# Seven half-width block products in place of eight for the gate and up projections of a decoder layer

## The chip, the cores and the metric

The kernel runs on one core of one Trainium2 chip. The metric is the device time of one execution in microseconds (us). The engines are TensorE (PE, with its weight loads PEld), VectorE (DVE), ScalarE (ACT), GpSimd (POOL) and SyncE (SP, which here issues DMAs).

## The reference, cut to what matters

One decoder layer on 512 tokens of 1024 features, in float32. Two of its stages are SwiGLU feed-forward blocks with 2816 hidden features; between them lie a projection, two mixers and an output projection, which the change does not touch.

```python
def swiglu_ffn(x, w13, w2):
    gate, up = jnp.split(x @ w13, 2, axis=-1)
    return (jax.nn.silu(gate) * up) @ w2

x = layer_norm(alpha * x + 0.5 * swiglu_ffn(x, ffn1_w13[i], ffn1_w2[i]), ln1_g[i], ln1_b[i])
h = x @ w_in[i]
...
x = layer_norm(alpha * x + mix @ w_out[i], ln2_g[i], ln2_b[i])
ple = jax.nn.sigmoid(x @ ple_gate_w[i]) * (p[i] @ ple_proj_w[i])
x = layer_norm(alpha * x + 0.5 * swiglu_ffn(x, ffn2_w13[i], ffn2_w2[i]) + ple, ln3_g[i], ln3_b[i])
```

## The kernel before, in words

Every float32 operand is split into a high part (a copy rounded to the matmul's input format, on ACT) and a low part (the difference, on DVE); `split` (lines 152 to 154) does this. A product is then three matmuls into one PSUM bank: high x high, high x low, low x high (`mm3`, lines 188 to 192). The input x stands transposed in XH and XL, eight k-tiles of 128 features by 512 tokens.

`ffn` (line 243) runs over 22 hidden tiles of 128 features in groups of 4, 6, 6 and 6. For each tile it makes a gate product and an up product, each 8 k-tiles x 3 matmuls with 512 tokens moving, into PSUM tags a and c (three banks each); `glu` applies silu on ACT, multiplies on DVE and splits the hidden tile. In the first stage's first group the k loop is outside (`k_outer`), so that work starts with the first weights. After a group the second product runs over four token blocks and two halves of 512 output columns: one unit is n x 3 matmuls (n tiles in the group) into PSUM tag b (two banks), and DVE adds it to the residual RES (line 304). After the last group each token block is normalised (`norm_natural`), and in the first stage turned back into XH and XL (`norm_turn`).

Weights come as units of 512 KB through `load` (line 156): SP issues the DMA into one of three raw buffers, ACT copies the high part, DVE subtracts the low part. `ahead` loads the next unit of the list wa (and the four wide ones, wd) whenever one has been used, four units deep; `side` loads one row block of the second product's weights into one of six buffers. Each engine has its own queue and takes its instructions in the order that is fixed when the kernel is built; that order follows the code but is not the code's own, as instructions that would wait are passed by others. In the second stage the gate products of the per-layer embedding (`gate`, `project`) come first.

Of the kernel before, what the change touches and what calls it, by code (L numbers as in the profile page):

```python
# [8 lines left out]
F32 = mybir.dt.float32  # L9
# [7 lines left out]
P = 128  # L17
# [6 lines left out]
GROUPS = [4, 6, 6, 6]  # L24
# [21 lines left out]
WD_AT = KT + 2 * (NF - GROUPS[0])  # L46
# [63 lines left out]
class Layer:  # L110
    def __init__(self, ctx, tc, wa, wb, wd, xT, xn, pT, cst, lvm, convw, vec, gb, out):
        self.tc, self.nc = tc, tc.nc
        self.wa, self.wb, self.wd, self.xT, self.xn, self.pT = wa, wb, wd, xT, xn, pT
# [21 lines left out]
        self.na = self.nb = 0  # L135
        self.ready = []

# [18 lines left out]
    def load(self, pool, tag, src, pieces=1):  # L156
        nc = self.nc
        width = PITCH if tag == "u" else 1024
        m = src.shape[-1]
        r = self.rawp.tile([P, PITCH], F32, name=self.nm("raw"), tag="raw")[:, 0:m]  # L160
        hi = pool.tile([P, width], F32R, name=self.nm("wh"), tag=tag + "h")[:, 0:m]
        lo = pool.tile([P, width], F32R, name=self.nm("wl"), tag=tag + "l")[:, 0:m]
# [9 lines left out]
    def ahead(self, pieces=1):  # L172
        d = self.na - WD_AT
        if 0 <= d < 4:
            self.ready.append(self.load(self.hlp, "u", self.wd[d], pieces))
        elif self.na < self.wa.shape[0] + 4:
            self.ready.append(self.load(self.hlp, "u", self.wa[self.na if d < 0 else self.na - 4], pieces))
        self.na += 1
# [3 lines left out]

    def side(self, pool, tag):
        r = self.load(pool, tag, self.wb[self.nb])
        self.nb += 1
        return r
# [56 lines left out]
    def ffn(self, zone, k_outer, evac_first, natural, turn):  # L243
        tc, act, dve = self.tc, self.nc.scalar, self.nc.vector
        w2p = zone.enter_context(tc.tile_pool(name=self.nm("w2p"), bufs=6))
        hp = zone.enter_context(tc.tile_pool(name=self.nm("hp"), bufs=7))
        sp = zone.enter_context(tc.tile_pool(name=self.nm("sp"), bufs=2))
        XH, XL = self.XH, self.XL

        def glu(pg, pu):  # L250
            s = sp.tile([P, S], F32, name=self.nm("sg"), tag="sg")
            act.activation(s, pg, AF.Silu)  # L252
            dve.tensor_tensor(s, s, pu, ALU.mult)
            hh = hp.tile([P, S], F32R, name=self.nm("hh"), tag="hh")
            hl = hp.tile([P, S], F32R, name=self.nm("hl"), tag="hl")
            self.split(hh, hl, s)
            return hh, hl

        for gi, n in enumerate(GROUPS):
            hs, w2 = [], []  # L260
            if gi == 0 and k_outer:
                accs = [(self.ps("a"), self.ps("c")) for _ in range(3)] + [(self.ps("b"), self.ps("b"))]
                for k in range(KT):
                    k_outer(k)
                    wh, wl = self.take()
                    for f in range(n):
                        for u in range(2):
                            c = (f * 2 + u) * P
                            self.mm3(accs[f][u], wh[:, c:c + P], wl[:, c:c + P], XH[:, k, :], XL[:, k, :],
                                     k == 0, k == KT - 1)  # L270
                    self.ahead()
                for f in range(n):
                    hs.append(glu(*accs[f]))
                for f in range(n):
                    w2.append(self.side(w2p, "w2"))
            else:
                for f in range(n):
                    pair = []
                    for u in range(2):
                        wh, wl = self.take()  # L280
                        pq = self.ps("ac"[u])
                        for k in range(KT):
                            self.mm3(pq, wh[:, k * P:(k + 1) * P], wl[:, k * P:(k + 1) * P], XH[:, k, :],
                                     XL[:, k, :], k == 0, k == KT - 1)
                        self.ahead()
                        pair.append(pq)
                    hs.append(glu(*pair))
                    w2.append(self.side(w2p, "w2"))
            last = gi == len(GROUPS) - 1
            for t in range(NT):  # L290
                tk = slice(t * P, (t + 1) * P)
                cuts = [0, 512, 1024]
                if last and not turn and t == NT - 1:
                    cuts = [0, 512, 768, 1024]
                for lo, hi in zip(cuts[:-1], cuts[1:]):
                    pd = self.ps("b")[:, 0:hi - lo]
                    for f in range(n):
# [769 lines left out]
```

## Time and profile before

| | |
|---|---|
| median of 3 runs | 1117.39 us (1116.77 to 1117.60) |
| the profiled execution | 1117.68 us, span 1115.9 us |
| PE busy | 1097.6 us, 98% of the span, 5193 matmuls |
| DVE busy | 524.6 us, 47% |
| ACT busy | 368.7 us, 33% |
| POOL busy | 115.3 us, 10% |
| DMA | 105.75 MB, mean 95 GB/s |

The span runs from the first to the last instruction. Busy time is the time in which an engine executed something; matmuls are pipelined, so the distance between the starts of two matmuls, not the duration of one, says how fast PE goes. A granted clock of 1.00 is TensorE at its upper level of 2.4 GHz. An engine's idle time is put down to what released it.

### The profile page before, as it was taken

To read this page: it belongs to the slowest core of one execution; us is meant where nothing else is said; L and a number is where in the kernel's file an instruction comes from. 1 tells how busy PE (TensorE), PEld (TensorE's weight loads), DVE (VectorE), ACT (ScalarE), POOL (GpSimd) and SP (SyncE) were. 2 spreads that over 40 slices of the span, in tenths; PEclk is the share of its full clock that TensorE was granted. 3 is DMA by queue.
4 is the path that set the end of the run, shared out by engine and by line. 5 is a ranking of instruction groups with operands and counts; after the bars stand their busy time and mean duration, and the time that the engine had idled before them with its cause. 6 is when DMAs were issued, how large, how long until landed. Compare 5 with 4: busy or idle time off the path is not lost.

```text
span 1115.9 us, 13126 instructions
## 1 busy us (share of the span) xinstructions
PE 1097.6 (98%) x5193; PEld 899.5 (81%) x5193; DVE 524.6 (47%) x822; ACT 368.7 (33%) x642; POOL 115.3 (10%) x189
## 2 busy tenths in 40 slices
PE   9999999999999999999999999999999999999996
PEld 7888888888888978778866877888888888888885
DVE  4534423432446366457674659454434324423435
ACT  4513302320341266323466533424123203402300
POOL 2000000000002202432111204100000000000013
PEclk9999999999999999999999999999999999999998
DMA  9524402431440042123110221524224314402302
GB/s 331 187 95 132 148 23 95 138 107 38 132 146 26 1 132 77 40 75 85 58 57 1 76 76 57 182 89 143 97 76 135 111 38 133 142 29 95 113 1 76
DMA packets 38061, 105.75 MB, mean 95 GB/s; under 512 B 10160, under 2 KB 12096, under 8 KB 38000
## 3 DMA queue, kind: packets, MB, share of 16 engines
q1 hardware_dynamic: 31776, 96.71, 27.0%
q0 software_dynamic: 1808, 6.04, 1.6%
q10 hardware_dynamic: 4416, 2.16, 0.7%
q8 instruction: 41, 0.67, 0.2%
q14 instruction: 20, 0.16, 0.1%
HBM read 102.41 MB, written 2.49 MB: 94 GB/s over the span
## 4 chain that ended last, share of the span: by engine, by line
PE 93%; DVE 2%; ACT 2%; POOL 1%; issue 1%; DMA 1%; POOLq 0%; ACTq 0%; DVEq 0%
PE pb L190 13%; PE pb L191 13%; PE pb L192 13%; PE pc L190 7%; PE pc L191 7%; PE pc L192 7%; PE pa L190 7%; PE pa L191 7%; PE pa L192 7%; PE pc L795 2%; PE pa L728 1%; PE pc L814 1%; DVE wl L154 1%; DMA raw<-in_wa_dram 1%; PE pa L507 1%
## 5 line engine op out<-in xcount | busy, mean ns | idle before, releaser
L153 ACT CAST wh<-raw 128x1024 fp32r<-128x1024 f32 (+2 forms) x181 | 186.6, 1035 | 473.0 <-PE pb L192 117.8
L154 DVE TENSOR_TENSOR wl<-raw,wh 128x1024 fp32r<-128x1024 f32 (+2 forms) x181 | 218.4, 1211 | 215.3 <-ACT wh L153 213.5
L190 PE MATMUL pb<-wh,hh 128*128 128x512 f32 (+1 forms) x358 | 138.4, 387 | 0.0
L191 PE MATMUL pb<-wl,hh 128*128 128x512 f32 (+1 forms) x358 | 138.0, 386 | 0.0
L192 PE MATMUL pb<-wh,hl 128*128 128x512 f32 (+1 forms) x358 | 138.0, 386 | 0.0
L190 PE MATMUL pa<-XH,wh 128*128 128x512 f32 x344 | 134.2, 390 | 0.0
L190 PE MATMUL pc<-XH,wh 128*128 128x512 f32 x344 | 134.1, 390 | 0.0
L191 PE MATMUL pa<-XL,wh 128*128 128x512 f32 x344 | 133.9, 389 | 0.0
L192 PE MATMUL pa<-XH,wl 128*128 128x512 f32 x344 | 133.8, 389 | 0.0
L191 PE MATMUL pc<-XL,wh 128*128 128x512 f32 x344 | 133.8, 389 | 0.0
L192 PE MATMUL pc<-XH,wl 128*128 128x512 f32 x344 | 133.8, 389 | 0.0
L190 PE MATMUL pb<-wh,XH 128*128 128x512 f32 (+2 forms) x288 | 110.4, 383 | 1.2 <-DVE RES L911 0.5
L191 PE MATMUL pb<-wl,XH 128*128 128x512 f32 (+2 forms) x288 | 106.1, 368 | 0.5 <-DVE wl L154 0.4
L192 PE MATMUL pb<-wh,XL 128*128 128x512 f32 (+2 forms) x288 | 106.2, 369 | 0.0
L304 DVE TENSOR_TENSOR RES<-RES,pb 128x512 f32<-128x512 f32 (+1 forms) x49 | 33.1, 676 | 114.5 <-PE pb L192 114.5
L206 POOL TENSOR_SCALAR bnrs<-bnmv 128x1 f32<-128x1 f32 x12 | 7.1, 590 | 733.4 <-DVE bnmv L204 733.4
L190 PEld LDWEIGHTS pb<-wh,hh 128*128 128x128 f32 x358 | 67.3, 188 | 14.2 <-ACT sg L252 0.3
L192 PEld LDWEIGHTS pb<-wh,hl 128*128 128x128 f32 x358 | 67.2, 188 | 13.6 <-DVE hl L154 0.3
L191 PEld LDWEIGHTS pb<-wl,hh 128*128 128x128 f32 x358 | 67.3, 188 | 13.4
L190 PEld LDWEIGHTS pa<-XH,wh 128*128 128x128 f32 x344 | 64.7, 188 | 14.0 <-ACT wh L153 0.6
L190 PEld LDWEIGHTS pc<-XH,wh 128*128 128x128 f32 x344 | 64.8, 188 | 13.5
L192 PEld LDWEIGHTS pa<-XH,wl 128*128 128x128 f32 x344 | 64.8, 188 | 13.4
(233 smaller groups left out, 1448.3 us busy)
## 6 DMA issues: line engine op xcount, KB each, us to landing
raw<-in_wa_dram SPq DMA_DIRECT2D x127, 512.0 KB, 3.6
raw<-in_wb_dram SPq DMA_DIRECT2D x46, 512.0 KB, 3.4
raw<-in_wd_dram SPq DMA_DIRECT2D x4, 520.0 KB, 4.1
RES<-in_xn_dram POOLq DMA_DIRECT2D x4, 512.0 KB, 10.6
gb<-in_gb_dram POOLq DMA_DIRECT2D x8, 256.0 KB, 5.9
xr<-in_xT_dram ACTq DMA_DIRECT2D x7, 256.0 KB, 4.6
TT<-in_gb_dram POOLq DMA_DIRECT2D x4, 256.0 KB, 3.7
out_dram<-RES SPq DMA_DIRECT2D x4, 256.0 KB, 2.1
```

Of the source, the lines that this page charges most:

```text
L153: self.nc.scalar.copy(hi, src)
L154: self.nc.vector.tensor_tensor(lo, src, hi.bitcast(F32), ALU.subtract)
L190: pe.matmul(o, wh, xh, start=first, stop=False)
L191: pe.matmul(o, wh, xl, start=False, stop=False)
L192: pe.matmul(o, wl, xh, start=False, stop=last)
L206: pool.tensor_scalar(rs[:, 1:2], mv[:, 1:2], float(eps), None, ALU.add)
L304: dve.tensor_tensor(rj, rj, pd, ALU.add)
L507: pe.transpose(dst[:, h * P:(h + 1) * P], src[:, h, :], ident)
L728: pe.matmul(pt[:, h * P:(h + 1) * P], MP[:, 0, c, h, :], TT[:, c, h, :], start=True, stop=True)
L795: pe.matmul(sc[m], DQT[r, h, t * P:(t + 1) * P], DKT[r, h, 0:n], start=True, stop=False)
L814: pe.matmul(po[:, 0:P], at[:, c * P:(c + 1) * P], DV[:, c, h, :], start=c == 0, stop=c == t)
```

## The change: what it does, and the diff

**Block products.** x is cut into four quarters: two halves of the tokens (256 each) by two halves of the features (four k-tiles each). For one hidden tile the weights are cut likewise: gate or up by half of the features (b11 and b12 belong to the first half of the features, b21 and b22 to the second). Gate and up for all tokens are eight block products of quarter by weight; Strassen's scheme in Winograd's form makes them from seven, of sums of quarters (s1, s2, s4, and one that takes the place of a quarter in XH) with sums of weights (t1 to t4). One product (`product`) is 4 k-tiles x 3 matmuls with 256 tokens moving. `head` makes the first product of the next tile within the body of the present one; `body` makes the other six, combines them on DVE, applies silu in two halves on ACT and splits the hidden tile. This is done for 18 tiles of the first stage (the first four stay as they were, "plain") and for all 22 of the second.

**Weights.** `blocks` loads the two 512 KB units of a tile, makes the sums on DVE and splits them, in seven steps that `ahead` calls one at a time during the tile before and that wait for the places at which the buffers are free. For b21 and b22 the low part isn't made by DVE: ACT writes the negative of the high part, and a DMA on POOL's queue adds the weights from DRAM to it. `load_add` does the same for the second product's weights, which now come in halves of 512 columns (256 KB), six buffers, two raw buffers of their own. The last group's second half-columns go into the buffers of the weight sums and are loaded after the last body.

**Groups and order.** The groups are 4, 3, 4, 3, 4, 4 and 3, 4, 4, 3, 4, 4. A group's second product comes behind the first body of the next group and runs over the half-columns first, then over the tokens; the last group's runs over the tokens first. The sums of x come from the raw input in the first stage (`combine_raw`) and from XH and XL, between the gate products, in the second (`combine`). The wide units and those behind them are no longer loaded before the last body is over.

```diff
-GROUPS = [4, 6, 6, 6]
+PLAIN = 4
+GROUPS1 = [4, 3, 4, 3, 4, 4]
+GROUPS2 = [3, 4, 4, 3, 4, 4]
+HALF = S // 2
+W2BUFS = 6
+PLAN = [("plain", KT), ("blocks", NF - PLAIN), ("wide", 4), ("plain", 40), ("blocks", NF)]
...
+    def load_add(self, pool, tag, src, rawp, bufs=None):
+        nc = self.nc
+        m = src.shape[-1]
+        r = rawp.tile([P, m], F32, name=self.nm("raw"), tag="raw")
+        hi = pool.tile([P, m], F32R, name=self.nm("wh"), tag=tag + "h", bufs=bufs)
+        lo = pool.tile([P, m], F32R, name=self.nm("wl"), tag=tag + "l", bufs=bufs)
+        nc.sync.dma_start(r, src)
+        nc.scalar.copy(hi, r)
+        nc.scalar.activation(lo, hi.bitcast(F32), AF.Copy, scale=-1.0)
+        nc.gpsimd.dma_start(lo, src, accum_op=ALU.add)
+        return hi, lo
...
+    def blocks(self, i, r, rec):
+
+
+        nc = self.nc
+        act, dve, pool = nc.scalar, nc.vector, nc.gpsimd
+        yield lambda: self.heads > r - 2
+        tp = self.tp
+        raw = [self.rawp.tile([P, PITCH], F32, name=self.nm("raw"), tag="raw")[:, 0:1024] for _ in range(2)]
+        for q in range(2):
+            nc.sync.dma_start(raw[q], self.wa[i + q])
+        b12, b11 = raw[0][:, 0:512], raw[0][:, 512:1024]
+        b21, b22 = raw[1][:, 0:512], raw[1][:, 512:1024]
+
+        def pair():
+            return [self.hlp.tile([P, PITCH], F32R, name=self.nm("w" + x), tag="u" + x)[:, 0:1024] for x in "hl"]
+
+        h, l = pair()
+        rec["b11"] = h[:, 0:512], l[:, 0:512]
+        self.split(*rec["b11"], b11)
+        yield lambda: self.bodies > r - 2
+        h, l = pair()
+        act.copy(h, raw[1])
+        act.activation(l, h.bitcast(F32), AF.Copy, scale=-1.0)
+        pool.dma_start(l, self.wa[i + 1], accum_op=ALU.add)
+        rec["b21"] = h[:, 0:512], l[:, 0:512]
+        rec["b22"] = h[:, 512:1024], l[:, 512:1024]
+
+        def total(a, b):
+            t = tp.tile([P, 512], F32, name=self.nm("tr"), tag="tr", bufs=3)
+            dve.tensor_tensor(t, a, b, ALU.add)
+            return t
+
+        def high(t):
+            h, l = [tp.tile([P, 512], F32R, name=self.nm("t" + x), tag="t" + x, bufs=5) for x in "hl"]
+            act.copy(h, t)
+            return h, l
+
+        def low(t, hl):
+            dve.tensor_tensor(hl[1], t, hl[0].bitcast(F32), ALU.subtract)
+
+        def after(n):
+            return lambda: self.bodies >= r or (self.bodies == r - 1 and self.place >= n)
+
+        yield lambda: self.bodies > r - 2
+        t1 = total(b12, b11)
+        t2 = total(t1, b22)
+        rec["t2"] = high(t2)
+        yield after(1)
+        t3 = total(b12, b22)
+        rec["t3"] = high(t3)
+        low(t2, rec["t2"])
+        yield after(3)
+        rec["t1"] = high(t1)
+        low(t3, rec["t3"])
+        yield after(4)
+        low(t1, rec["t1"])
+        t4 = total(t2, b21)
+        rec["t4"] = high(t4)
+        yield lambda: True
+        low(t4, rec["t4"])
+        rec["done"] = True
...
+    def plan_weights(self):
+
+        n = d = 0
+        self.recs = []
+        for kind, count in PLAN:
+            for _ in range(count):
+                if kind == "blocks":
+                    rec = {}
+                    self.recs.append(rec)
+                    yield from self.blocks(n, len(self.recs) - 1, rec)
+                    n += 2
+                elif kind == "wide":
+                    yield lambda: self.bodies == len(self.recs)
+                    self.plain(self.wd[d])
+                    d += 1
+                else:
+                    yield lambda: self.bodies == len(self.recs)
+                    self.plain(self.wa[n], 4 if n == 0 else 1)
+                    n += 1
...
+    def combine_raw(self, k, upper, lower):
+
+        dve = self.nc.vector
+        x11, x21 = upper[:, 0:HALF], upper[:, HALF:S]
+        x12, x22 = lower[:, 0:HALF], lower[:, HALF:S]
+
+        def put(pair, v):
+            self.split(pair[0][:, k], pair[1][:, k], v)
+
+        dve.tensor_tensor(x22, x21, x22, ALU.subtract)
+        dve.tensor_tensor(x21, x11, x21, ALU.subtract)
+        put(self.sums["s1"], x22)
+        dve.tensor_tensor(x11, x22, x11, ALU.subtract)
+        put(self.quarter(1, 0), x21)
+        dve.tensor_tensor(x12, x12, x11, ALU.add)
+        put(self.sums["s2"], x11)
+        put(self.sums["s4"], x12)
+
...
+        def side(must=False):
+            i = count["loaded"]
+            if i == len(items):
+                return
+            g, j, f = items[i]
+            end = g == last and j == 1
+            if self.bodies < rec0 + nf if end else i - W2BUFS >= count["freed"]:
+                assert not must
+                return
+            src = self.wb2[first_f + f, j]
+            pool, tag, bufs = (tp, "t", 5) if end else (self.w2p, "w2", None)
+            w2[f, j] = self.load_add(pool, tag, src, self.w2r, bufs)
+            count["loaded"] += 1
+
...
+        def second(g, t, j, cuts):
+            fs = range(start[g], start[g + 1])
+            tk = slice(t * P, (t + 1) * P)
+            for lo, hi in cuts:
+                pd = self.ps("b")[:, 0:hi - lo]
+                for f in fs:
+                    while (f, j) not in w2:
+                        side(True)
+                    self.mm3(pd, hs[f][0][:, tk], hs[f][1][:, tk], w2[f, j][0][:, lo:hi], w2[f, j][1][:, lo:hi],
+                             f == fs[0], f == fs[-1])
+                rj = self.RES[t][:, j * 512 + lo:j * 512 + hi]
+                if g == 0:
+                    evac_first(rj, pd, t, j)
+                else:
+                    dve.tensor_tensor(rj, rj, pd, ALU.add)
+            if t == NT - 1:
+                count["freed"] += len(fs)
...
+        def head(f):
+            rec = self.need(rec0 + f, "b11")
+            pq = self.ps("a")[:, 0:HALF]
+            product(pq, self.quarter(0, 0), rec["b11"])
+            p1 = self.scratch("p1", HALF)
+            act.copy(p1, pq)
+            state[f] = rec, p1
...
+            def step(n):
+                self.place = n
+                if extra:
+                    extra.pop(0)()
+                if feed:
+                    self.ahead()
+                    if n in (2, 5):
+                        side()
+
...
+            p26 = self.ps("a")
+            product(p26[:, HALF:S], self.sums["s2"], rec["t2"])
+            step(1)
+            product(p26[:, 0:HALF], self.quarter(0, 1), rec["b21"])
+            w = self.scratch("part", 5 * HALF).rearrange("p (a b) -> p a b", b=HALF)
+            s = self.scratch("sg", S)
+            dve.tensor_tensor(w[:, 0:2], halves(p26), bc(p1, 1, 2), ALU.add)
+            act.activation(s[:, 0:HALF], w[:, 0], AF.Silu)
+            step(2)
+            p7 = self.ps("c")[:, 0:HALF]
+            product(p7, self.quarter(1, 0), rec["t3"])
+            dve.tensor_tensor(w[:, 2], p7, w[:, 1], ALU.add)
+            step(3)
+            p5 = self.ps("c")[:, 0:HALF]
+            product(p5, self.sums["s1"], rec["t1"])
+            dve.tensor_tensor(w[:, 3:5], bc(p5, 1, 2), w[:, 1:3], ALU.subtract)
+            step(4)
+            if f + 1 < nf:
+                head(f + 1)
+            step(5)
+            p43 = self.ps("c")
+            product(p43[:, 0:HALF], self.quarter(1, 1), rec["t4"])
+            step(6)
+            product(p43[:, HALF:S], self.sums["s4"], rec["b22"])
+            dve.tensor_tensor(w[:, 2:4], halves(p43), w[:, 2:4], ALU.add)
+            act.activation(s[:, HALF:S], w[:, 2], AF.Silu)
+            dve.tensor_tensor(halves(s), halves(s), w[:, 3:5], ALU.mult)
+            hidden(f, s)
+            self.bodies += 1
+            self.place = 0
+            if feed:
+                self.ahead()
+
...
+        for g in range(1 if plain else 0, len(groups)):
+            for f in range(start[g], start[g + 1]):
+                body(f, not extra, extra)
+                extra = []
+                if f == start[g] and g > 0:
+                    second_group(g - 1)
```

## Rows read from the trace of the kernel before

**Rows 1.** The page's chain of waits, share of the span by engine.

```profile
PE 93%; DVE 2%; ACT 2%; POOL 1%; issue 1%; DMA 1%; POOLq 0%; ACTq 0%; DVEq 0%
```

**Rows 2.** Busy time by stage; columns stand in the first line.

```profile
core 0: us, PE busy (x) PEld busy (x) DVE busy (x) ACT busy (x) POOL busy (x), PEclk, DMA share, GB/s
...
6.00:46.00 40.00, 40.00 (x175) 33.09 (x176) 18.72 (x29) 16.76 (x25) 7.66 (x14) 1.00 0.80 289
46.00:366.00 320.00, 320.00 (x1419) 264.62 (x1418) 136.30 (x161) 87.74 (x111) 9.72 (x15) 1.00 0.31 99
...
392.00:700.00 308.00, 301.14 (x1575) 236.68 (x1574) 194.45 (x417) 146.36 (x353) 74.67 (x121) 1.00 0.22 68
700.00:755.00 55.00, 55.00 (x248) 45.42 (x247) 27.17 (x32) 22.30 (x27) 3.09 (x6) 1.00 0.41 135
755.00:1106.00 351.00, 351.00 (x1566) 291.26 (x1565) 136.18 (x159) 85.76 (x107) 11.15 (x15) 1.00 0.28 91
```

**Rows 3.** Timeline of PE near the end; start us, duration us, engine, line, operation.

```profile
1100.31 0.39 PE L192 MATMUL pb<-wh,hl 128*128 128x512 f32 x1
...
1101.67 0.39 PE L192 MATMUL pb<-wh,hl 128*128 128x512 f32 x1
1101.90 0.28 PE L190 MATMUL pb<-wh,hh 128*128 128x256 f32 x1
...
1105.85 0.28 PE L190 MATMUL pb<-wh,hh 128*128 128x256 f32 x1
```

**Rows 4.** Timeline of PE in the value projection.

```profile
384.75 0.28 PE L190 MATMUL pb<-wh,XH 128*128 128x256 f32 x1
...
387.10 0.28 PE L192 MATMUL pb<-wh,XL 128*128 128x256 f32 x1
387.22 0.28 PE L190 MATMUL pb<-wh,XH 128*128 128x264 f32 x1
...
390.01 0.28 PE L192 MATMUL pb<-wh,XL 128*128 128x264 f32 x1
```

**Rows 5.** Costliest groups by form; busy us, mean ns, idle before.

```profile
L154 DVE TENSOR_TENSOR wl<-raw,wh 128x1024 fp32r<-128x1024 f32 x173 | 211.8, 1229 | 207.2 <-ACT wh L153 205.5 <-PE pb L192 0.2
L153 ACT CAST wh<-raw 128x1024 fp32r<-128x1024 f32 x173 | 180.7, 1049 | 458.8 <-PE pb L192 117.8 <-PE pc L191 107.2 <-PE pa L191 93.5
...
L154 DVE TENSOR_TENSOR hl<-sg,hh 128x512 fp32r<-128x512 f32 x44 | 30.0, 685 | 1.4 <-ACT hh L153 1.4
...
L153 ACT CAST hh<-sg 128x512 fp32r<-128x512 f32 x44 | 27.0, 615 | 11.7 <-DVE sg L253 11.7
L252 ACT ACTIVATE sg<-pa 128x512 f32<-128x512 f32 x43 | 25.3, 590 | 5.7 <-PE pa L192 5.7
...
L714 DVE SCALAR_TENSOR_TENSOR MP<-pa,g,ta 128x256 f32<-128x256 f32 x16 | 6.8, 477 | 10.1 <-PE pa L710 10.1
...
L562 ACT COPY DV<-pb 128x256 f32<-128x256 f32 x8 | 3.0, 371 | 14.3 <-PE pb L192 12.5 <-POOL RES L217 1.8
```

**Rows 6.** Timeline of all engines, two passes back to back on ACT and DVE.

```profile
381.24 1.08 ACT L153 CAST XH<-pa 128x512 fp32r<-128x512 f32 x2
...
381.86 1.29 DVE L154 TENSOR_TENSOR XL<-pa,XH 128x512 fp32r<-128x512 f32 x2 [7.07 <-ACT XH L153]
```

**Rows 7.** Timeline of PE in the second product of the first group.

```profile
53.19 0.41 PE L190 MATMUL pb<-wh,hh 128*128 128x512 f32 x1
53.44 0.40 PE L191 MATMUL pa<-XL,wh 128*128 128x512 f32 x1
```

**Rows 8.** POOL's costliest groups: one issue of a DMA.

```profile
L240 POOL DMA_DIRECT2D TT<-in_gb_dram x4 | 2.3, 579 | 15.0 <-PE pa L728 15.0
```

**Rows 9.** DMA issues: KB each, median us to landing.

```profile
RES<-in_xn_dram POOLq DMA_DIRECT2D x4, 512.0 KB, 10.6
gb<-in_gb_dram POOLq DMA_DIRECT2D x8, 256.0 KB, 5.9
...
TT<-in_gb_dram POOLq DMA_DIRECT2D x4, 256.0 KB, 3.7
```

More of the change, by code (lines that the diff above doesn't have):

```diff
@@ L134, in __init__ @@
         self.ident = self.CST[:, C_ID:C_ID + P]
-        self.na = self.nb = 0
+        self.nb = self.heads = self.bodies = self.place = 0
         self.ready = []
+        self.weights = self.plan_weights()
+        self.may = next(self.weights)
     def nm(self, s):
@@ new lines, in plain @@
+    def plain(self, src, pieces=1):
+        self.ready.append(self.load(self.hlp, "u", src, pieces))
+    def blocks(self, i, r, rec):
[50 more added lines that the diff above has]
+        rec["done"] = True
@@ L180, in take, with ahead, need @@
+    def ahead(self):
+        if self.may and self.may():
+            self.may = next(self.weights, None)
     def take(self):
         return self.ready.pop(0)
+    def need(self, r, part):
+        while len(self.recs) <= r or part not in self.recs[r]:
+            assert self.may()
+            self.ahead()
+        return self.recs[r]
     def side(self, pool, tag):
-        r = self.load(pool, tag, self.wb[self.nb])
+        r = self.load(pool, tag, self.wb[self.nb], width=1024)
         self.nb += 1
@@ L240, in load_gb @@
             self.nc.gpsimd.dma_start(tiles[j], src.partition_broadcast(P))
[L243 to L255, printed above, removed]
-            self.split(hh, hl, s)
[L257 to L270, printed above, removed]
-                    self.ahead()
[L272 to L293, printed above, removed]
-                    cuts = [0, 512, 768, 1024]
-                for lo, hi in zip(cuts[:-1], cuts[1:]):
-                    pd = self.ps("b")[:, 0:hi - lo]
-                    for f in range(n):
-                        self.mm3(pd, hs[f][0][:, tk], hs[f][1][:, tk], w2[f][0][:, lo:hi], w2[f][1][:, lo:hi],
-                                 f == 0, f == n - 1)
-                    rj = self.RES[t][:, lo:hi]
-                    if gi == 0:
-                        evac_first(rj, pd, t, lo // 512)
-                    else:
-                        dve.tensor_tensor(rj, rj, pd, ALU.add)
-                if last:
-                    natural(t, cuts)
-                    if turn and t:
-                        turn(t - 1)
@@ L335, in first_ffn @@
             fetch_x(0)
-            self.split(self.XH[:, 0, :], self.XL[:, 0, :], xr[0])
-            self.ahead(4)
+            split_x(0)
+            self.ahead()
             fetch_x(1)
-            for _ in range(3):
+            split_x(1)
+            for k in range(1, 4):
                 self.ahead()
-            lv = gp.tile([P, 512], F32, name="lvraw")
-            lam = gp.tile([P, 256], F32, name="lam")
+                fetch_x(k + 1)
+            lv = self.scratch("sg", S)
+            ll = self.scratch("part", 5 * HALF)
+            lam, jl = ll[:, 0:HALF], ll[:, HALF:S]
             def small_loads():
@@ L392, in second_ffn @@
         with ExitStack() as zone:
[L393 to L394 removed]
+            self.open_sums(zone)
             with ExitStack() as z2:
@@ L436, in second_ffn @@
                         wp = [self.side(pp, f"wp{k}") for k in range(2)]
-                        self.load_gb(gbt, G_LN3)
-                    gate(t, 1, wg)
-                for j in range(2):
-                    for t in range(NT):
-                        project(t, j)
+                    if t == 2:
+                        self.norm_turn(NT - 1)
+                    gate(t, 0, wg)
+                for _ in range(2):
+                    next(sums)
+                wg = [self.take() for _ in range(4)]
+                for t in range(NT):
+                    gate(t, 1, wg)
+                    project(t, 0)
+                    for _ in range(2):
+                        next(sums, None)
+                for _ in sums:
+                    pass
+                for i in range(2):
+                    self.split(*self.quarter(1, 0, 2 * i, 2), hold[i])
+                for t in range(NT):
+                    self.ahead()
+                    project(t, 1)
+                    self.ahead()
             def first(rj, pd, t, j):
```

240 lines of the change are left out of this document (177 added, 63 removed).

## The prediction

> **What bounds the kernel now.** I read the page's chain of waits first: TensorE (PE) carries 93% of the chain that ended last, DVE and ACT 2% each [rows 1]. Then the busy time by stage [rows 2]: in both feed-forward stages (46 to 366 us, 755 to 1106 us) PE is busy for the whole stretch at a granted clock of 1.00, the upper level, while DVE is busy 39 to 43% and ACT 24 to 27%. DMA has room: 0.31 and 0.28 of the engines' time. Only the start is different: DMA share 0.80 with 289 GB/s. The mixers between, 392 to 700, lose 6.9 us of PE, which the change does not touch. So in the two stages time is PE's matmul count times its spacing, and the change is worth what it takes off that product, until another engine becomes late.
>
> **Spacing of a matmul.** Six starts of 512 columns lie between 1100.31 and 1101.67 us: 0.2267 us each. From 1101.90 to 1105.85 there are 33 steps of 256 columns: 0.1197 [rows 3]. In the value projection 20 steps of 256 columns take 2.35 us: 0.1175, and 23 steps of 264 columns 2.79: 0.1213 [rows 4]. So half the columns cost 52 to 53%, and a weight load for each half-wide matmul is still hidden. I take 0.1185, the middle of the two 256-column series.
>
> **What PE gains.** A hidden tile (128 columns of gate and of up, 512 tokens) is 2 x 8 x 3 = 48 matmuls of 512 columns: 48 x 0.2267 = 10.88 us. As seven block products it is 7 x 4 x 3 = 84 of 256 columns: 84 x 0.1185 = 9.95 us. The saving is 0.93 us per tile; 18 tiles of the first stage (four stay plain) and 22 of the second make 40: **37.0 us**. With 0.1175 it is 40.4, with 0.1197 33.0, with the dearest row (0.1213) 27.6. The second products keep their 528 matmuls of 512 columns per stage, so nothing is gained or lost there on PE.
>
> The Trainium skill speaks against this step: "TensorE: Matmul & The Clock Gate", section "Back-to-back issue gap", gives for a stream of weight load and matmul about 131 ns at 512 columns and 81 ns at 128. An estimate on a straight line between them is 98 ns at 256, so 84 x 98 = 8.2 against 48 x 131 = 6.3 us, and the change would lose 77 us. The trace disagrees at both widths (227 and 118 ns), and the measurement decides.
>
> **What DVE and ACT get.** Durations [rows 5]: DVE 0.685 us for 512 elements, 1.229 for 1024, 0.477 for 256; ACT 0.615 for 512, 1.049 for 1024, 0.371 for 256, silu 0.590. Back to back two DVE passes of 512 take 1.29, so 0.60 a step, two ACT passes 1.08 [rows 6].
> - Before, one tile costs DVE 3 x 1.229 + 2 x 0.687 = 5.1 us.
> - After, the weights of a tile need nine 512-wide DVE passes (four sums, five low parts: b11, t1 to t4) = 9 x 0.60 = 5.4, the combining of the products five 512-wide (about 0.69 each, as each waits for something) and one 256-wide = 3.9. Together 9.3 us in a body of 9.95 us of PE.
> - ACT: five 512-wide copies 2.7, b21/b22 high and negative 2.1, p1 and two half silus 1.1, hidden 0.6: 6.5, plus 1.2 for each half of a second-product weight; with two of those in a body 8.9.
>
> Both come near PE in bodies that follow each other (three or four at a time), and have slack again in a second product (8 units of 12 x 0.2267 = 2.72 us with one DVE add each). What decides is whether they wait for each other. Issued in the code's order, DVE waits within a body for the high part of t4 (0.6), for the half silu (0.4) and for the hidden copy (0.65): 9.4 + 1.7 = 11.1 us; with the two half loads standing in ACT's queue ahead of the copies that DVE waits for, 2.4 more: 13.5. Either is over PE's 9.95. But the order on the engines is not the code's: at 53 us PE alternates a second product (pb) with the next gate product (pa), which the code issues one after the other [rows 7]. Instructions that wait are passed by others. Below, nothing is lost; above, 34 us (rival A). I am nearer the lower end, since in that same stretch before the queues were filled around the waits: 4 us.
>
> **What the adding DMA gets.** Per block one of 512 KB for b21/b22 (POOL queue), per tile two of 256 KB. Such a DMA is not in the trace. POOL issues plain ones in 0.58 us [rows 8]; 256 KB land in 3.7 us (5.9 when DMA is full), four 512 KB at once in 10.6 [rows 9]. Issuing costs POOL 1.7 us per tile, and it is idle there (9.7 us of 320, [rows 2]). Traffic per tile rises from 1.5 to 2.5 MB in 15.4 us, 162 GB/s against 289 reached at the start.
> - b21/b22: its buffer comes free when the last product of body r ends and is needed by the second product of body r+2, 9.95 + 1.42 us later. ACT takes 2.1, POOL 0.6: the DMA may take 8.7 us. By the nearest single row it does; I price it at nothing (bounds: below 8.7 nothing, at 10.6 rival B).
> - Second-product weights: six buffers, but groups of four tiles need eight halves. The last two come free while the fourth unit of the first half-columns runs and are wanted 3.4 us later; copy 0.6, negative 0.6, POOL 0.6 and landing 3.7 make 5.5: a wait of 2.1 us in each of six such groups, 12 us (none if PE runs the next tile's products meanwhile, as in [rows 7]; 26 us at 5.9 us of landing). I take half, 6. The first half-columns and both stages' last group load earlier or beside a body; SP's queue holds block loads behind the half loads (two raw buffers), with 3.6 us to land and a body of time, at no cost.
>
> The skill's "DMA: Bandwidth & Descriptors", section "Anatomy of one DMA", has about 2.0 us plus bytes at 436 GB/s for such a DMA, an estimate of 2.6 us at 256 KB; by it the full wait would be 6 x 1.0 = 6 us. No run here shows it yet, nor the price of the adding.
>
> **The seams.**
> - End of stage one: a group of four gives each token block 5.44 us of PE where six gave 8.16, and DVE needs some ten passes of 0.60 = 6.0 for its adds, statistics, normalisation and splits; the four wide value units (4 x 1.23) now fall there too. DVE falls behind by 4 x 0.6 + 4.9 = 7, and the next stage's first two token blocks (96 matmuls x 0.1197 = 11.5 us) hide most: 3 us (0 to 10).
> - Start of stage two: the sums of x cost DVE about 24 passes, 14 us, spread over the gate products of 55 us where DVE was busy for 27 [rows 2]: 2 us (0 to 5).
> - Start of stage one: 12 us more of DVE in 40 where 18.7 were busy; 3 MB of half weights come earlier beside a DMA share of 0.80. PE asks for 512 KB per 5.4 us, 1.7 us of transfer at 289 GB/s: 0 (to 6).
>
> **Sum.** The profiled execution took 1117.68 us (span 1115.9 and 1.8 around it), 0.3 over the median. 1117.7 - 37.0 + 4 + 6 + 3 + 2 = 1095.7, against the median **1095 us**.
>
> **Rivals.**
> - A, other side: DVE and ACT wait for each other in runs of bodies. The point is a body period of 10.88 us; above it a tile is dearer than before. By the code's order it is 11.1 to 13.5. PE sees it at the second product behind a run, where two PSUM buffers give it 5.4 us before DVE's first add must be done: DVE is 9 to 10 us late after four bodies (wait 4.2), 8 after three (3.0). Six and three such runs: 34 us. With all 12 of the half weights and 6 of seams: 1117.7 - 37 + 34 + 12 + 6 = **1133**. For it: DVE at 94% of a body. Against: the passing in [rows 7].
> - B: the adding DMA of 512 KB lands after 8.7 us. At 10.6, 1.9 x 40 = 76 us come back: **1157**. For it: that row. Against: it is of four at once at a DMA share of 0.80.
> - C: everything hides: 1117.7 - 40.4 to - 33.0 = 1077 to 1085, **1081**.
> - D: the block products do not run at 0.1185; even at 0.1295, where 84 equal 48, nothing is gained: **1117 or more** with the seams. No row is above 0.1213.
>
> **Numbers.** Forecast (1082 to 1108) 0.56; C 0.17; A 0.16, of which a third ends between 1108 and 1120; B 0.06; D and no change 0.05. 0.2%, 2.2 us, is what can be told from no change. Faster 0.75, same 0.03, slower 0.22. Range 1078 to 1130: below it part of C, above it half of A, and B. The likeliest case alone has 1082 to 1108.
>
> **What would show it.** Right: about 3360 matmuls of 256 columns 0.1175 to 0.120 us apart, PE busy for over 96% of both stages, each shorter by 12 to 20 us; DVE near 70% in them. A shows as PE idle behind DVE's RES add at the start of a second product; half weights as PE waiting for a wl in it; B as PE waiting for a DMA at a body's second product; the seam as waits at the first values after stage one. I am wrong if the spacing is above 0.125, or if PE idles over 40 us in the two stages.

## The result, and the profile after

The changed kernel took 1150.58 us (median of 4 runs, 1148.54 to 1157.21) against 1117.49: ratio 1.0307 [1.0264, 1.0351]. It is 33 us slower where 22 us faster were forecast, and lies outside the range of 1078 to 1130. Its profiled execution took 1148.54 us, span 1146.8 (before 1115.9).

First the page: the chain of waits, which answers to [rows 1], PE's own busy group with the longest wait, and the DMA issues that the change added.

```profile
PE 67%; DMA 10%; issue 8%; DVE 8%; ACT 4%; POOL 3%; SPq 0%; POOLq 0%; ACTq 0%; DVEq 0%
...
L295 PE MATMUL pb<-wl,hh 128*128 128x512 f32 (+1 forms) x356 | 144.5, 406 | 24.4 <-DMA wl<-in_wb_dram 24.3
...
wl<-in_wb_dram POOLq DMA_DIRECT2D x88, 256.0 KB, 6.0
wl<-in_wa_dram POOLq DMA_DIRECT2D x40, 512.0 KB, 7.0
```

PE had 93% of the chain and now has 67%. One wait stands out: 24.3 us for the low parts of second-product weights (wl from in_wb), inside second products (pb<-wl,hh). In the kernel before, the same group waited for nothing:

```profile
L191 PE MATMUL pb<-wl,hh 128*128 128x512 f32 (+1 forms) x358 | 138.0, 386 | 0.0
```

Then busy time by stage, with the columns of [rows 2]: start and plain tiles, rest of stage one, mixers, gates, stage two.

```profile
6.00:57.00 51.00, 47.11 (x192) 37.75 (x191) 32.89 (x69) 30.96 (x59) 11.47 (x17) 0.93 0.86 276
57.00:381.00 324.00, 308.89 (x2048) 284.11 (x2049) 209.32 (x341) 170.10 (x285) 57.78 (x72) 0.98 0.66 155
408.00:720.00 312.00, 302.25 (x1566) 236.11 (x1565) 196.41 (x415) 142.67 (x349) 74.67 (x121) 0.99 0.22 67
720.00:768.00 48.00, 47.41 (x214) 39.01 (x213) 40.49 (x61) 26.59 (x38) 3.03 (x4) 1.00 0.40 122
768.00:1136.00 368.00, 352.14 (x2383) 325.76 (x2382) 237.17 (x390) 189.76 (x323) 68.00 (x83) 0.97 0.67 153
```

In both stages PE now stands idle (15.1 and 15.9 us) and its granted clock is below 1.00. The DMA engines are busy 0.66 and 0.67 of the time where they were 0.31 and 0.28 [rows 2].

The block products themselves, in PE's timeline (start us, duration us), answer to [rows 3, 4]:

```profile
166.58 0.28 PE L294 MATMUL pa<-s2h,th 128*128 128x256 f32 x1
...
167.78 0.28 PE L295 MATMUL pa<-s2l,th 128*128 128x256 f32 x1
```

Ten steps in 1.20 us: 0.1200 each, and 84 of them are 10.08 us for a body, where 48 x 0.2267 were 10.88. Now the six second products of four tiles, each a window from its first to its last matmul:

```profile
70.50:100.01 29.51, 24.98 (x100) 19.77 (x99) 9.53 (x15) 9.33 (x17) 4.72 (x6) 0.88 0.51 114
186.74:214.09 27.35, 23.85 (x100) 19.26 (x99) 7.91 (x12) 8.50 (x15) 4.51 (x6) 0.94 0.53 117
300.82:327.39 26.57, 23.81 (x100) 19.27 (x99) 7.90 (x12) 8.50 (x15) 4.08 (x5) 0.94 0.55 122
870.08:897.28 27.20, 24.06 (x100) 18.97 (x99) 7.91 (x12) 8.50 (x15) 4.50 (x6) 0.94 0.56 117
937.43:967.21 29.78, 24.80 (x100) 19.65 (x99) 7.90 (x12) 8.49 (x15) 4.52 (x6) 0.89 0.50 107
1053.94:1082.68 28.74, 25.26 (x100) 20.01 (x99) 7.97 (x12) 8.51 (x15) 4.51 (x6) 0.88 0.53 111
```

Each has 96 matmuls of 512 columns, 96 x 0.2267 = 21.76 us. The windows are 169.15 us together, and each reaches 0.16 us into the next body, whose first matmul starts before the last one of the window has ended (213.92 against 214.09 in the second). So from one start to the next they take 168.2 us where 130.6 are needed: 37.6 us lost. Of these 169.15 - 146.74 = 22.4 are idle (146.74 is PE's busy time in the six); the other 15 are matmuls at the lower clock. The second window, followed through the timelines of ACT, POOL and PE (the start time in front tells the order):

```profile
195.81 0.62 ACT L184 CAST wh<-raw 128x512 fp32r<-128x512 f32 x1 [5.90 <-PE pb L296]
196.47 0.63 ACT L185 ACTIVATE wl<-wh 128x512 fp32r<-128x512 f32 x1
...
197.39 0.87 POOL L186 DMA_DIRECT2D wl<-in_wb_dram  x1 [10.02 <-PE pb L296]
...
203.35 0.50 PE L295 MATMUL pb<-wl,hh 128*128 128x512 f32 x1 [3.50 <-DMA wl<-in_wb_dram]
...
204.71 0.63 PE L294 MATMUL pb<-wh,hh 128*128 128x512 f32 x1
205.14 0.63 PE L295 MATMUL pb<-wl,hh 128*128 128x512 f32 x1
...
208.03 0.39 PE L295 MATMUL pb<-wl,hh 128*128 128x512 f32 x1
208.26 0.39 PE L296 MATMUL pb<-wh,hl 128*128 128x512 f32 x1
```

ACT waits 5.90 us for PE to let go of the buffer, copies and negates, POOL issues, and PE waits 3.50 us more. Soon behind the wait matmuls start 0.43 us apart (the lower level of the clock) until 207.5, then 0.23 again. The granted clock, the third number from the end, shows it:

```profile
203.60:207.50 3.90, 3.90 (x11) 3.04 (x11) 0.69 (x1) 0.08 (x1) 0.86 (x1) 0.56 1.01 220
207.50:214.00 6.50, 6.50 (x30) 5.36 (x30) 1.37 (x2) 1.85 (x4) 0.34 (x1) 1.00 0.08 15
```

Where the 30.9 us between the two spans went, by such windows of both traces:

| Part | us |
|---|---|
| 40 tiles, 10.88 to 10.08 us | -32.0 |
| six second products of four tiles | +37.6 |
| start: first block product at 58.9, four plain tiles were done at 50.2 before (52.25 less nine matmuls of 0.2267) | +8.7 |
| last second product of stage one, 25.1 for 21.8 us of matmuls (before none over) | +3.3 |
| mixers, first value projection to gates: 334.4 to 339.6 | +5.2 |
| gates and first four bodies of stage two | +4.2 |
| last second product of stage two, 25.7 for 21.9 | +3.6 |
| behind the last matmul, 9.5 to 9.8 | +0.3 |

They add up to 30.9.

### The profile page after: what moved, and what is told of

Same layout as the page of the kernel before. It is cut to its first block, busy times and chain, and to the rows that moved or that the text cites. A ratio compares the mean times of both kernels' runs of the same rounds, so it can differ in the third digit from the quotient of the medians.

```text
span 1146.8 us, 17686 instructions
## 1 busy us (share of the span) xinstructions
PE 1089.9 (95%) x6627; PEld 953.1 (83%) x6627; DVE 731.2 (64%) x1306; ACT 571.0 (50%) x1076; POOL 226.2 (20%) x317
## 3 DMA queue, kind: packets, MB, share of 16 engines
q0 software_dynamic: 20240, 50.09, 24.2%
## 4 chain that ended last, share of the span: by engine, by line
PE 67%; DMA 10%; issue 8%; DVE 8%; ACT 4%; POOL 3%; SPq 0%; POOLq 0%; ACTq 0%; DVEq 0%
PE pb L295 9%; PE pb L294 9%; PE pb L296 9%; PE pc L294 6%; PE pc L295 6%; PE pc L296 6%; PE pa L296 4%; PE pa L294 4%; PE pa L295 4%; DMA wl<-in_wb_dram 4%; DMA raw<-in_wa_dram 3%; PE pc L1110 2%; DVE wl L160 2%; DMA raw<-in_wb_dram 2%; ACT wh L159 1%
## 5 line engine op out<-in xcount | busy, mean ns | idle before, releaser
L295 PE MATMUL pb<-wl,hh 128*128 128x512 f32 (+1 forms) x356 | 144.5, 406 | 24.4 <-DMA wl<-in_wb_dram 24.3
L230 DVE TENSOR_TENSOR tl<-tr,th 128x512 fp32r<-128x512 f32 x160 | 109.5, 686 | 58.1 <-ACT th L226 56.6
L160 DVE TENSOR_TENSOR wl<-raw,wh 128x1024 fp32r<-128x1024 f32 (+3 forms) x97 | 95.7, 993 | 50.8 <-ACT wh L159 50.0
L226 ACT CAST th<-tr 128x512 fp32r<-128x512 f32 x160 | 97.5, 613 | 45.9 <-PE pc L295 33.5
L294 PE MATMUL pa<-XH,wh 128*128 128x256 f32 (+1 forms) x344 | 100.7, 293 | 3.7 <-ACT part L423 2.2
L159 ACT CAST wh<-raw 128x1024 fp32r<-128x1024 f32 (+3 forms) x97 | 81.2, 844 | 45.2 <-DMA raw<-in_wa_dram 22.5
L295 PE MATMUL pa<-XL,wh 128*128 128x256 f32 (+1 forms) x344 | 100.8, 293 | 2.1 <-DVE XL L160 2.1
L296 PE MATMUL pa<-XH,wl 128*128 128x256 f32 (+1 forms) x344 | 100.7, 293 | 1.7 <-DMA wl<-in_wa_dram 1.7
L296 PE MATMUL pc<-XH,tl 128*128 128x256 f32 x320 | 91.0, 284 | 0.0
L294 PE MATMUL pc<-XH,th 128*128 128x256 f32 x320 | 91.0, 284 | 0.0
L295 PE MATMUL pc<-XL,th 128*128 128x256 f32 x320 | 91.0, 284 | 0.0
```

The lines of the kernel that those rows point to most:

```text
L159: self.nc.scalar.copy(hi, src)
L160: self.nc.vector.tensor_tensor(lo, src, hi.bitcast(F32), ALU.subtract)
L226: act.copy(h, t)
L230: dve.tensor_tensor(hl[1], t, hl[0].bitcast(F32), ALU.subtract)
L294: pe.matmul(o, wh, xh, start=first, stop=False)
L295: pe.matmul(o, wh, xl, start=False, stop=False)
```

## Experiments

Each compares with the kernel before on the same chip. Further down, a second product of four tiles is short when it takes about 21.9 us.

**e1_sub: half weights that are loaded out of a second product, by DVE.**

```diff
     def load_add(..., sub=False):
         nc.sync.dma_start(r, src)
+        if sub:
+            self.split(hi, lo, r)   # ACT copy, DVE subtraction
+            return hi, lo
...
     def second_group(g):
-                        side()          # at three places
+                        side(sub=True)
```

> Half columns that are loaded out of the second products get their low parts by DVE's subtraction (about 0.7 us) instead of ACT's negation and the adding DMA (0.6 + 0.87 + 5.9 us); those loaded beside a body stay as they are. Theory, late halves: in a group of four the 7th and 8th halves may only be written when the 1st and 2nd are free, and the adding DMA makes them land some 8 us after that. Then the six second products of four tiles return from 26.6 to 29.8 us to about 21.8, the 24.3 us of PE waits for wl from in_wb fall below 5, the clock stays at 1.00 there, and the time is 1112 us (1108 to 1120), under the kernel before. Rival, raw halves late: the raw loads (4.4 us, two buffers) are what is late, and the low part only comes after; then the waits move to ACT or DVE and the time stays at 1140 to 1150. Rival, DVE too full: the subtractions push back the sums of the next body; then waits for tl appear and the time is 1120 to 1140.

Measured 1132.85 us, ratio 1.0133 [1.0102, 1.0163]: half of the 33 us are gone, the forecast of 1112 was missed. From e1's view of PE's waits (total us, times, longest), the line that was 24.3, 10, 3.5 in the changed kernel:

```profile
PE pb L298 <- DMA wl<-in_wb_dram: 13.6, 8, 2.2
```

Each of the six still has one wait, for the 8th half, which is asked for in another place and still took the adding DMA. Windows of two of the six:

```profile
183.81:207.80 23.99, 22.24 (x100) 18.11 (x99) 9.89 (x15) 6.72 (x12) 1.91 (x3) 1.00 0.41 100
1036.87:1062.92 26.05, 23.86 (x100) 19.28 (x99) 9.90 (x15) 6.71 (x12) 1.91 (x3) 0.93 0.40 94
```

A wait of 1.75 us in the first left the clock at 1.00, one of 2.19 us in the other was followed by the lower level; the 2.06 us between the windows are more than the 0.44 us between the waits. The other four waited 1.87 to 2.21 us and stayed at 1.00, so the length of a wait alone does not tell whether the clock falls.

**e5_sub_all: the 8th half too.**

```diff
                     while (f, j) not in w2:
-                        side(True)
+                        side(True, True)
```

> As e1_sub, and the 8th half of a group of four, which e1_sub still loaded with the adding DMA because it is asked for only where its product is issued, gets its low part by DVE too. Theory, late halves: the one wait of about 2 us left in each of the six second products goes, they take 21.8 to 22.3 us each instead of 24.0 to 26.1, and the time is 1132.9 - 14 = 1119 us (1115 to 1123). Rival, raw halves late: the 8th half's raw load (issued with the 7th's, two raw buffers) then lands too late itself, a wait of 1 to 2 us for DVE's wl takes the place and the time is 1126 to 1133.

Measured 1117.64 us (10 runs), ratio 1.0007 [0.9997, 1.0017]. All six are short, at full clock; two of them:

```profile
180.74:202.69 21.95, 21.95 (x100) 18.20 (x99) 10.49 (x16) 6.09 (x11) 1.07 (x2) 1.00 0.38 98
1027.46:1049.42 21.96, 21.96 (x100) 18.20 (x99) 10.49 (x16) 6.10 (x11) 1.07 (x2) 1.00 0.38 98
```

With 44 of the 88 adding DMAs of half weights still there, 32.9 us are gone. Neither the raw loads nor DVE took the place.

**e2_threes: no waiting half instead of a quicker one.**

```diff
-GROUPS1 = [4, 3, 4, 3, 4, 4]
-GROUPS2 = [3, 4, 4, 3, 4, 4]
+GROUPS1 = [4, 3, 3, 3, 3, 3, 3]
+GROUPS2 = [3, 3, 3, 3, 3, 3, 4]
```

> Groups of at most three tiles behind the first one of stage one (4,3,3,3,3,3,3) and before the last one of stage two (3,3,3,3,3,3,4); nothing else differs. Theory, late halves: six buffers then hold both half columns of a group, so of the six slow second products only stage one's first (7.7 us over its matmul time) and the tail's stay: 1150.6 - 31 = 1120 us (1114 to 1127). Rival, adding DMA too slow in any case (q0 moves 50 MB now against 6 before): the groups of three wait as well, for halves that are written when the group before lets them go; then PE still waits over 15 us for wl from in_wb, and the time is 1135 to 1155.

Measured 1123.29 us, ratio 1.0052 [1.0037, 1.0067]. The same line of e2's waits (they stand in stage one's first second product, which is still of four tiles, and in the last of each stage):

```profile
PE pb L295 <- DMA wl<-in_wb_dram: 5.2, 4, 2.9
```

All adding DMAs are still there and land in 6.1 us, and a second product of three tiles takes 16.5 us for 16.3 of matmuls (all but the first of stage two, 20.6, and the last of each stage). So it is not that the adding DMA is slow in itself: six buffers for eight halves put it on the path. The same kernel taken again (e6_threes_all_late) gave 1120.27 in one run, under what was expected:

> A second look at the kernel of e2_threes, for its trace beside the next two: 1123.3 us (1122 to 1125).

**e4_copy: the price of the adding.**

```diff
-        nc.gpsimd.dma_start(lo, src, accum_op=ALU.add)
+        nc.gpsimd.dma_start(lo, src)
```

> The half columns' second DMA copies instead of adding, so their low parts hold the whole weights: the subtraction is left out, and the time tells what the adding costs. Theory, adding is dear: POOL's issue falls from 0.88 to about 0.58 us and the landing from 6.0 to some 4.5 us as for SP's plain loads of the same size; the ten waits shrink by 1.8 us each with their share of clock, and the time is 1130 us (1122 to 1138). Rival, the queue is slow whatever it does: issue and landing stay within 0.3 us and the time at 1145 to 1152.

This kernel leaves the subtraction out. Measured 1132.36 us (one run), 18 us less than the changed kernel. POOL's group of these issues, busy us and mean ns, and the landing, both of e4_copy; the changed kernel has 878 ns and 6.0 us:

```profile
L186 POOL DMA_DIRECT2D wl<-in_wb_dram x88 | 47.0, 535 | 287.6 <-PE pb L296 133.0
...
wl<-in_wb_dram POOLq DMA_DIRECT2D x88, 256.0 KB, 4.3
```

The adding costs 1.7 us of landing; 0.34 of them are POOL's, as landing is counted from the start of the issue (197.39 + 5.9 = 203.3 in the window above). The waits fell to 14.2 us.

**e3_late_first: stage one's first halves later.**

```diff
-                    if k in (0, 1, 2):
+                    if k in (5, 6, 7):
                         side()
```

> The six half columns that stage one loads beside its first three k steps are loaded beside the last three instead. Theory, transfers set the start: the first 40 us move 13.4 MB at 340 GB/s, and 3 MB of it are these halves (raw and added), so the wide tiles of weights land 4 to 6 us earlier, the first four tiles end near 50 us instead of 56.7, and the time is 1144 us (1141 to 1147). Rival, DVE sets the start: it is busy 19.5 of the 20 us from 40 to 60 and its chain ends at the first block product; then the start moves by less than 2 us and the time is 1148 to 1152. If the halves then come too late for the first second product at 70, its 7.7 us of excess grow and the time rises above 1152.

Measured 1145.24 us, ratio 1.0240 [1.0195, 1.0285]; its interval overlaps the changed kernel's, so the trace has to tell. Its windows of the plain tiles and of what follows:

```profile
6.00:50.00 44.00, 43.50 (x192) 35.66 (x190) 32.14 (x69) 29.35 (x57) 11.29 (x17) 1.00 0.99 318
50.00:70.00 20.00, 16.91 (x113) 16.27 (x114) 17.22 (x28) 15.95 (x26) 1.72 (x2) 0.91 0.58 133
```

The 192 plain matmuls end at 49.5 instead of 56.7 us, where the kernel before had them done at 50.2: transfers set that. Then PE waits 3.59 us for the first Silu (2.22 in the changed kernel), with DVE busy 17 of 20 us; ahead of it on ACT stand a copy that waited 1.39 us for DVE's sums and the load of Silu's table, 1.28 us. At the end of the first second product 4.1 of the 7.2 us are left. Both theories have a part.

**e8_low_by_dve: DVE as full as it can be.**

```diff
-        act.activation(l, h.bitcast(F32), AF.Copy, scale=-1.0)
-        pool.dma_start(l, self.wa[i + 1], accum_op=ALU.add)
+        dve.tensor_tensor(l, raw[1], h.bitcast(F32), ALU.subtract)
```

> The low parts of b21 and b22, which ACT negates and an adding DMA completes (40 times 512 KB), come from one DVE subtraction of 1024 columns (1.2 us) instead; nothing else differs from the changed kernel. Theory, DVE is what the adding DMA spares: DVE's 9.3 us a body becomes 10.5, over PE's 10.08, so PE waits for tl or wl in each body, bodies take 10.5 to 10.8 us, and the time is 1150.6 + 40 x 0.5 = 1170 us (1160 to 1180); q0 moves 21 MB less. Rival, DVE has room (it was 98% busy only in windows of 10 us and never late): bodies stay at 10.1 us, the DMA engines get emptier, halves land sooner, and the time is 1135 to 1150.

Measured 1147.24 us (one run), inside the rival's range: my theory fell. Windows of one body each, the changed kernel's first, then e8's:

```profile
167.16:177.24 10.08, 10.08 (x86) 10.08 (x85) 8.89 (x16) 6.51 (x12) 0.86 (x2) 1.00 0.62 160
```

```profile
167.16:177.24 10.08, 10.08 (x87) 10.08 (x86) 10.04 (x17) 5.66 (x11) 0.00 (x0) 1.00 0.37 106
```

DVE at 10.04 of 10.08 us still makes PE wait for nothing; a body is 10.08 us in both. So b21 and b22 did not need the adding DMA for DVE's sake.

**e7_threes_sub_late: e2, e5 and e3 together.**

> Groups of at most three (e2_threes), the DVE subtraction for every half that is loaded out of a second product or asked for there (e5_sub_all), and stage one's first halves loaded beside its last k steps (e3_late_first). Theory, the three costs are separate and add up: e2_threes 1123.3, less 6.7 for stage one's first second product (28.5 to 21.8 us), less 4 to 5 for the start, is 1112 us (1108 to 1116), faster than the kernel before. Rival, they share a cause (all wait for the same DMA engines, so that one alone gives nearly all): 1118 to 1123.

Measured 1111.20 us, ratio 0.9941 [0.9924, 0.9957]: 0.6% faster than the kernel before, and the costs add up. PE no longer waits for a wl from in_wb at all.

**e9_no_add_b and e10_start_two: e7 with e8's edit, in all tiles and in the first three of stage two.**

```diff
+        if NF - PLAIN <= r < NF - PLAIN + 3:        # e10 only
+            dve.tensor_tensor(l, raw[1], h.bitcast(F32), ALU.subtract)
```

> e7_threes_sub_late with DVE subtracting the low parts of b21 and b22 in all 40 tiles (e8_low_by_dve's edit). e8 showed bodies of 10.1 us with DVE busy 10.0 of them, in runs of four. Theory, DVE has a body's room and no more: it falls behind by some 0.1 us a body, catches up in the second products, and the first bodies of stage two (16.7 to 21.3 us second product) get quicker as the DMA engines empty: 1107 to 1112 us, so the same as e7 or a little faster. Rival, the subtractions that e7 already gives DVE in its second products leave no time to catch up: sums come late at the start of the runs of bodies, and the time is 1114 to 1122.

> e7_threes_sub_late with that subtraction only in the first three tiles of stage two, where halves and blocks load at once (DMA engines busy over 90% from 765 to 805 us in the changed kernel) and the first second product takes 21.3 us for 16.3 us of matmuls. Theory, the DMA engines are what is short there, as e8's 17.8 us suggest: 3 to 4 us go, 1107.5 us (1106 to 1110). Rival, DVE's queue is (PE waits 2.9 us for the first sums into RES): then nothing goes or 1 to 2 us more are lost, 1110 to 1114.

Measured 1109.64 us, ratio 0.9923 [0.9908, 0.9937], and 1106.97 us, ratio 0.9896 [0.9877, 0.9915]. Against e7, e9's interval overlaps and e10's does not. The first second product of stage two, in e7 and then in e10:

```profile
789.19:810.49 21.30, 18.41 (x76) 14.74 (x75) 13.67 (x22) 8.14 (x14) 0.88 (x1) 0.92 0.46 112
```

```profile
790.16:807.96 17.80, 16.81 (x76) 13.61 (x75) 11.68 (x19) 6.80 (x13) 0.86 (x1) 1.00 0.50 126
```

3.5 us go there though DVE has more to do for the three tiles, as the theory had it. PE's wait for DVE's add into RES falls from 2.89 to 0.99 us. In e7 DVE had stood idle 4.97 us for ACT before it, and ACT 3.35 and 1.44 us for raw halves. That points to transfers; but the edit also takes a pass off ACT in each of the three tiles, and no run parts the two. e10 is 10.6 us under the kernel before, and not to be told from e9.

**e11_last_four and e12_silu_early: two more edits on e10.**

```diff
-GROUPS1 = [4, 3, 3, 3, 3, 3, 3]
+GROUPS1 = [4, 3, 3, 3, 3, 2, 4]                                  # e11, e12
+                        act.activation(..., AF.Silu)   # k == 6, e12 only
```

> e10_start_two with groups 4, 3, 3, 3, 3, 2, 4 in stage one, so that its last group has four tiles as in the changed kernel. Theory, cover at the seam: the norm of a token tile takes DVE and POOL some 6 us, a unit pair of three tiles lasts 4.1 us on PE and one of four 5.4; the seam's excess falls from 6.0 us (24.4 - 16.3 - 2.1) to 3.8 (27.6 - 21.8 - 2.0), 2 us less than e10. Rival, the group of two (six halves free, 4.1 us less cover for the loads) or the last group's late halves cost as much: no difference to e10 within 1 us.

> e11_last_four with one Silu of a single column on ACT behind the sums of constants at the sixth k step of stage one, so that the table that Silu needs is loaded before the first four tiles end. Theory: the 1.28 us of ACT without a tile ahead of the first Silu (L423 in the changed kernel's chain) goes from the path, PE's wait of 2.2 to 4.1 us for it shrinks by 1.3, and with it the loss of clock: 1 to 3 us less than e11. Rival, the wait is for DVE's products behind it: within 0.5 us of e11.

Measured 1107.09 us, ratio 0.9907 [0.9892, 0.9922], and 1106.54 us, ratio 0.9906 [0.9891, 0.9921]: both like e10, so neither forecast came true. In e11 PE waits 3.86 us for ACT's copy of the last hidden tile where the seam should have gained. In e12 the table is loaded early, and the first Silu is no earlier; ACT's timeline of e12, then of e11:

```profile
41.43 1.28 ACT L674 ACT_TABLE_LOAD   x1
...
51.38 0.62 ACT L232 CAST th<-tr 128x512 fp32r<-128x512 f32 x1 [1.08 <-DVE tr L227]
51.91 0.61 ACT L159 CAST wh<-raw 128x512 fp32r<-128x512 f32 x1
52.43 0.59 ACT L429 ACTIVATE part<-pa 128x512 f32<-128x512 f32 x1
```

```profile
49.95 0.61 ACT L159 CAST wh<-raw 128x512 fp32r<-128x512 f32 x1
50.58 1.28 ACT L429 ACT_TABLE_LOAD   x1
51.88 0.60 ACT L429 ACTIVATE part<-pa 128x512 f32<-128x512 f32 x1
```

In e12 a copy that waits for DVE's sums (tr) stands ahead of the Silu, so without the table it is held back by DVE through ACT's queue, and PE waits 3.3 us for it (2.6 in e11). As ACT's order changed with the edit, what either costs alone is not shown.

## Why the prediction was wrong, step by step

**The step that failed** is the half weights in "What the adding DMA gets": 6 us priced (12 for the full waits, 26 at most), 37.6 measured. Its mechanism was right and was named: eight halves, six buffers. Three sizes were wrong.
- The path from the freed buffer to the matmul: priced 0.6 + 0.6 + 0.6 + 3.7 = 5.5 us; measured from 195.81 to 203.35, 7.5 us. From the start of POOL's issue on it is 5.96 us where I had 0.6 + 3.7 = 4.3, from plain rows as the nearest. That counted POOL's 0.6 twice, as landing already holds the issue: it is 5.96 against 3.7, and e4_copy puts 1.7 of the 2.3 on the adding. The need came 4.0 us after the buffer (199.85 without the wait), not 3.4, so 3.5 us are waited and not 2.1. In the six groups this wait is 2.6 to 3.5 us, and in three of them a second one of 0.9 to 1.8 follows.
- Half of it was struck off, in the hope that PE would run other matmuls. It ran none: every wait stands in PE's timeline as idle.
- What a wait costs behind itself was not in the sum at all. The 22.4 us of waits lie within the 26 that I had as the most. Beside them 15.0 more went in the same windows (169.15 against e5's 131.73 for the six), at the lower clock. The Trainium skill says so in "TensorE: Matmul & The Clock Gate", section "HAM oscillation — how this bites in real kernels": a wait for a DMA between bursts of matmuls lets the clock fall, so the next burst begins slow. The changed kernel's trace agrees (granted clock 0.56 from 203.6 to 207.5, behind the wait of 3.50, and 0.88 to 0.94 in all six windows); e1's does not for five of its six waits (1.75 to 2.21 us, clock 1.00).

e1, e5 and e2 show the cause from two sides: a quicker low part or fewer halves, and the time goes. e5's six windows are 37.4 us shorter, its profiled execution only 30.9 (1148.54 to 1117.61): its last second product of stage one is 3.3 us longer (PE waits 4.1 us for ACT's hh there), its first bodies 1.5 us, and the stretch behind its last matmul 3.0 us (12.8 against 9.8); the rest is small. Six buffers were kept in every run; more of them were not tried.

**The other steps.**
- Spacing: 0.1185 taken, 0.1200 measured; the saving is 32.0 us, in the low part of its range (27.6 to 40.4), and rival D is false. I took the middle of two series, and the one from rows of the same inner loop (0.1197) was the right one.
- "What DVE and ACT get": 4 us priced, 0 measured in the runs of bodies behind the start. Rival A is false: bodies are 10.08 us even with DVE busy 10.04 (e8). The 9.4 us of DVE in its sum is the 9.3 worked out above it, which changes nothing.
- b21 and b22: priced at nothing, landing 7.0 us in the median (5.4 to 9.3), under the 8.7 that I had worked out; one wait of 1.7 us in 40, at the start of stage two. Rival B is false, although its 1157 is nearest to the result. Rival C is false too: even e10 is 26 us above its 1081.
- Start of stage one, priced 0 (to 6): 8.7 us. I held 3 MB of earlier loads to be free beside a DMA share of 0.80; e3 shows that they were not, and that DVE's sums, which I counted (12 us), then come out on the path, with the table load, for about 3 us.
- End of stage one 3 (0 to 10): 3.3 us. The number is right by luck: 1.9 us are PE's wait for a half weight of the last group (wl from in_wb, at 361.0), which I had at no cost, and only 0.5 a wait for POOL's normalised RES; the values behind it do not wait for DVE.
- Start of stage two 2 (0 to 5): 4.2 us, but 1.7 of them are the wait for b21/b22's adding DMA, with a granted clock of 0.87 from 800 to 813 behind it, while the DMA engines are busy 0.87 of the four bodies. e10's row points to transfers too; waits for DVE's sums of x do not show.
- The end of stage two was not in the sum: 3.6 us, of which PE waits 1.3 for ACT's hh and 1.2 for DVE's add into RES.
- The mixers, "which the change does not touch": 5.2 us. The offset between the traces grows inside the attention part (from about 15 us at 560 to 20 at 637 of the trace before), the clock is 0.91 from 620 to 640 of the trace after, and the matmuls come in another order though their code is the same. In e1 to e5 and e7 to e12 the same stretch takes 338.2 to 340.4 us, so the late halves are not its cause. The cause stays open.

By these sizes the sum would have been 1117.7 - 32.0 + 37.6 + 8.7 + 3.3 + 5.2 + 4.2 + 3.6 + 0.3 = 1148.6, against 1148.5 for the profiled execution. The test I had set, PE busy for over 96% of both stages, fails with 95.3% (308.89 of 324) and 95.7% (352.14 of 368). The other, PE idle for over 40 us in the two stages, did not fire (31.0 us): it leaves out what goes at the lower clock, in which PE counts as busy.

## What to carry to other kernels

When a loop is regrouped, count the buffers that one group needs against those there are: a load that may start only when an earlier part of the same group is done has its latency on the path, less the work that is left in between (7.5 us and 4.0 in the window above), and here that alone undid the arithmetic that was saved. Give such loads the shortest path (e5) or make the group fit (e2), and keep the slow path for loads with a body of time ahead of them. Price each wait of PE with what its clock may lose behind it: over the six windows 0.7 us for each us of waiting in the changed kernel, 0.6 in e4, 0.3 in e1.

## What the runs showed of the hardware

An adding DMA of 256 KB cost POOL 0.88 us to issue and landed 6.0 us after the issue began, the copy of the same bytes 0.54 and 4.3 (e4). The Trainium skill's "DMA: Bandwidth & Descriptors", section "Anatomy of one DMA — SWDGE (gpsimd) path", gives about 2.0 us plus the bytes at 436 GB/s for a DMA of this queue, an estimate of 2.6 us for 256 KB. The runs are above it with and without the adding, beside other transfers. The adding also fills the DMA engines: the added queue takes 24.2% of their time for 50.1 MB, and 19.9% when 88 of its transfers copy. And not every wait of PE was followed by the lower clock, nor did its length decide: in e1 the one of 2.19 us was, one of 2.21 was not; in e4 waits of 1.90 to 2.36 us were in four of the six windows (granted clock 0.93), those of 2.33 and 2.62 in the other two were not (1.00).
